# One load stream instead of two, query and key columns of group A sliced, and half of one modulation row after the routing

## The chip, the core and the metric

The kernel runs on one core of a Trainium2 chip. Its time is device microseconds of that core, the median of the runs shown. TensorE does the matmuls, VectorE (DVE), ScalarE (ACT) and GpSimd (POOL) the elementwise work, and SyncE (SP) issues the large loads.

## What is computed

A decoder layer on 256 tokens of 2048 features in float32: six modulation rows from c, a modulated RMSNorm, three groups of heads that share one input projection and one output projection, a second modulated norm, a mixture of 32 experts, a final norm.

```python
mod = (c_act @ ada_w[l] + ada_b[l])[:, None, :]
sh1, sc1, g1, sh2, sc2, g2 = jnp.split(mod, 6, axis=-1)
h = rmsnorm(x, norm1_g[l]) * (1.0 + sc1) + sh1
x = x + g1 * hybrid_mixer(h, w_in[l], ...)       # aq ak av | bq bk bv bz bb ba | cq ck cv, then @ w_out
h = rmsnorm(x, norm2_g[l]) * (1.0 + sc2) + sh2
x = x + g2 * hierarchical_moe(h, ...)            # group top-1, expert top-2 of 32
return rmsnorm(x, final_norm_g)
```

Group A is dilated attention (8 heads of 64), group B a gated delta rule (8 value heads of 128, with a causal convolution ahead of it), group C attention with sinks (8 heads, 2 key heads).

## The kernel before

All weights come in tiles of 128x2048 floats (1 MiB), each by one DMA that SP issues. A `Stream` (L114) holds a list of free slots in SBUF and a list of loads; a tile is loaded as soon as the program reaches a free slot, and tiles are used in the order of their loads. Each engine runs a fixed order, made at build time by a scheduler that takes instructions out of the program's order where it reckons that they are ready earlier; what stands earlier in the program goes first among ready ones.

Slices (L190 to L224, L298 to L388). The norm's two modulation rows sh1 and sc1 are made in six slices of 256 or 512 features (`ada_tile`, L298). A finished slice is turned into columns (`modulate`), x is normed and transposed into `hx` as a high and a low half (`input_rows`), and then the columns O_BQ to O_BZ of w_in are multiplied with this slice (`win_tile`, L357). Each weight tile is first split into halves: ACT casts it, DVE or POOL subtracts (`split`, L281). A product is three matmuls (`mm3`, L273). The first slice's result is copied to SBUF, those of the five later slices are added there by DVE (`evac`, L267). The 16 columns bb and ba are done with each slice as well (`gate_columns`), with the tokens stationary.

Pairs (L391 to L420). The other columns of w_in are done when all of `hx` is there: 256 columns in two tiles, with the sum kept in PSUM (`win_pair`). They are aq, ak, av, cq, ck, cv and bz; for av, bz and cv the tokens are stationary ("av", "tok"), for the others the weights ("chan").

Rows (L425 to L437). The other four modulation rows g1, sh2, sc2 and g2 need 16 tiles each (`row_tile`): eight matmul records per tile that share the array by column groups. `spread2` (L444) broadcasts a row over the partitions with two matmuls.

Two streams feed this: `st`, with three slots of its own plus one, carries slices, pairs and w_out, and after them the experts; `st2`, with the two slots of `side`, carries the rows (L453 to L482).

The middle (L936 to L953): the program has the delta rule (L676 to L884) first, then av, aq and ak with rows, attention A, the c columns with rows, attention C, the z columns with rows. Then x is loaded again, the delta rule's output is normed, gated and split (`delta_out`), and the output projection runs in two passes: tiles 0 and 3 of each column block (the attention groups) with the last rows, then tiles 1 and 2 (the delta rule's heads). The second pass also broadcasts g2 into `g2b` (L981 to L983), norms for the router and makes the logits.

Routing (L1031 to L1061) is a chain of small DVE operations, two matmuls for the slots' positions, and the gather of the first experts' tokens. The experts (L1239 on) then take 24 tiles a pair. From L943 on slots come free in steps: `side` and ring2's four give nine in all, ring3 gives three (after the output projection), the two tiles h2 (the routed rows before their split) two more.

Of the kernel before, what the change touches and what calls it, by code (L numbers as in the profile page):

```python
# [18 lines left out]
NB = 2  # L19
# [19 lines left out]

PAIRS = [c for a, e in ((O_AQ, O_BQ), (O_CQ, N_IN), (O_BZ, O_BB)) for c in range(a, e, 256)]  # L40

EARLY = ([("ada", s, k0, nk, q) for k0, nk in SLICES for s in range(2) for q in range(nk)]
         + [("b", k0, nk, c) for k0, nk in SLICES for c in range(O_BQ, O_BZ, 2048 // nk)]
         + [("pair", c, h) for c in PAIRS for h in range(2)]
# [4 lines left out]
def hybrid_moe(ctx: ExitStack, tc: tile.TileContext, x, c, norm1_g, norm2_g, early, ada_w, ada_b, w_bb,  # L49
# [129 lines left out]
    T.transpose(pt[:, 0:KT], csg, ident[0:KT, 0:KT])  # L179
    V.tensor_copy(csil[:, :, 3], pt[:, 0:KT])  # L180


# [21 lines left out]
    def win_items(j):  # L204
        k0, nk = SLICES[j]
        return [(early_load("b", k0, nk, c), lambda t, a=(k0, nk, c): win_tile(*a)(t)) for c in range(O_BQ, O_BZ, 2048 // nk)]

# [18 lines left out]
    for nk, r in ((4, 4), (2, 8)):  # L226
# [6 lines left out]
        for k0, n in SLICES:  # L233
            if n == nk:
# [21 lines left out]
    for tag, m0, n in CH:  # L256
        t = ep_tile(tag, n)
        for i in range(n):
            chan[m0 + i] = (t, i)
    av = ep.tile([P, NB, 512], F32, name="av", tag="av")  # L260
    tok = ep.tile([P, NB, 1024 + 16 + 128], F32, name="tok", tag="tok")
# [95 lines left out]
    def win_tile(k0, nk, c0):  # L357

        def chans(w, cc, m):

            h = hs[k0]
            p = bank("w")
            for u in range(2):
                for kt in range(nk):
                    mm3(p[:, 256 * u:256 * u + 256], [x[:, kt, cc + P * u:cc + P * (u + 1)] for x in w],
                        [x[:, kt] for x in h], kt == 0, kt == nk - 1)
            t, i = chan[m]
            evac(t[:, i:i + 2].rearrange("p m b t -> p (m b t)"), p, k0)

        def gate_columns():  # L370
            h = hs[k0]
            for b in range(NB):
                p = bank("w")
                for kt in range(nk):
                    mm3(p[:, 0:16], [x[:, kt, P * b:P * (b + 1)] for x in h], [x[:, k0 // P + kt] for x in wbb],
                        kt == 0, kt == nk - 1)
                evac(tok[:, b, K_BB:K_BB + 16], p[:, 0:16], k0)

        def f(t):
            t = t.rearrange("p (k n) -> p k n", k=nk)  # L380
            n = 1024 // nk
            for a in range(0, 2048 // nk, n):
                w = split(t[:, :, a:a + n], nk, 0)
                for z in range(0, n, 256):
                    chans(w, z, 8 + (c0 - O_BQ + a + z) // P)
            if c0 == O_BQ:
                gate_columns()
        return f  # L388
# [34 lines left out]
    rowp = {}  # L423

    def row_tile(i, kt):  # L425
        def f(t):
            if kt == 0:
                rowp[i] = bank("r", name="prow2")
            for g in range(4):
                mm(rowp[i][32 * g:32 * g + 32, :], csil[:, kt, 3 - i:35 - i], t[:, 512 * g:512 * (g + 1)],  # L430
                   start=(kt == 0), stop=(kt == 15))
            if kt == 15:
# [17 lines left out]

    rows_q = [(ada_rows(i, kt), row_tile(i, kt)) for i in range(4) for kt in range(KT)]

    st2 = Stream()  # L453

# [13 lines left out]
    rows_q = on(st2, rows_q)  # L468
    a_cols, c_cols, z_cols = ([x for c0 in range(a, e, 256) for x in on(st, win_pair(c0))]
                              for a, e in ((O_AQ, O_BQ), (O_CQ, N_IN), (O_BZ, O_BB)))  # L470
# [104 lines left out]
    st.retire(*spare)  # L575
    for s in side:
        st.retire(s, to=st2)
    st.grow((wk, "rx"))
# [13 lines left out]

    def swap_keys():
        kd = wk.tile([P, NB, P], F32, name="kswap")
# [67 lines left out]
    def attention(grp):  # L662
# [3 lines left out]
        for j in range(2):  # L666
            ms = (2 * j, 2 * j + 1)
            sd = [attn_scores(grp, m) for m in ms]
# [7 lines left out]
    def delta():  # L676
        def f4(t):
# [21 lines left out]

        conv(0)  # L700
        conv(1)

        bb = tok[:, :, K_BB:K_BB + 8]
        ba = tok[:, :, K_BB + 8:K_BB + 16]
# [77 lines left out]
        for b, hs, ts in units:  # L782
            p = bank("d")
            mm(p, identr, never[:, None, :].to_broadcast([P, 4, P]), start=True, stop=False)
            for i in range(4):
                h = hs.start + i
                mm(p[:, P * i:P * (i + 1)], gg[:, b, h:h + 1].to_broadcast([P, P]), tri, start=False, stop=True)
                S.activation(qk[:, b, h], p[:, P * i:P * (i + 1)], AF.Exp, bias=ngc[:, b, h:h + 1], scale=1.0)
        conv(2)
        conv(3)  # L790
        for b in range(NB):
            for q in range(2):
                tokens(vtok[:, b, 4 * q:4 * q + 4], cv[2 + q], b)
        R = [ep.tile([P, 8, P], F32, name="R", tag=f"bv{b}") for b in range(NB)]
        for b, hs, ts in units:
# [14 lines left out]
            V.tensor_tensor(Um[:, b, hs], ident[:, None, :].to_broadcast([P, 4, P]), Um[:, b, hs], op=ALU.subtract)  # L810
            transposed(Tm, Um, b, hs)
        for l in range(1, 7):

# [7 lines left out]
            for b, hs, _ in units:  # L821
# [18 lines left out]
            if l < 6:  # L840
                for b, hs, _ in units:
                    transposed(Um, Tm, b, hs)


# [357 lines left out]
    def squares(n):  # L1202
        for b in range(NB):
            if n == 3 and b:
                y = mp.tile([P, 1024], F32, name="sqv", tag="yal", bufs=1)[:, 0:512]
                V.scalar_tensor_tensor(y, x1[n][:, b], 0.0, x1[n][:, b], op0=ALU.add, op1=ALU.mult, accum_out=ss3[:, b, n:n + 1])
# [4 lines left out]
    def new_y(dt, s):  # L1211
        return tuple(mp.tile([P, 1024], dt, name=f"y{h}{s}", tag=f"y{h}{s}", bufs=1) for h in "ab")

# [23 lines left out]
    sl.gather_all()  # L1237
    behind = []
    for e in range(0, NE, 2):  # L1239
# [12 lines left out]
        if e == NE - 2:  # L1252
            hT.append(turned(1, hid[1]))
            break
        yh, yl = new_y(F32R, "h"), new_y(F32R, "l")
        for u in range(2):
# [16 lines left out]

    ys = new_y(F32, "h")
    for n in range(4):
# [13 lines left out]
    with tc.For_i(0, nov, 1):  # L1289
# [24 lines left out]
        sl.back(0)  # L1314
        ys = new_y(F32, "h")
        G.memset(ys[0][64:128], 0.0)
# [86 lines left out]
```

## Time and profile before

| | us |
|---|---|
| median of 3 runs | 1645.95 (1643.81 to 1646.33) |
| the profiled execution | 1645.27 |
| its span, first to last instruction | 1643.4 |
| TensorE busy | 1545.9 (94%) |
| VectorE, ScalarE, GpSimd busy | 672.1, 398.6, 182.8 |
| DMA | 573.76 MB, 349 GB/s over the span |

Times below are us from the start of the span. A busy TensorE is one with a matmul in flight; since matmuls overlap, the sum of single durations is more than the busy time. An idle time is put down to what ended it.

### The profile page before, as it was taken

What the parts mean: (1) busy time and instruction counts of PE and PEld (TensorE: products, weight loads), DVE (VectorE), ACT (ScalarE), POOL (GpSimd) and SP (SyncE); (2) the same over time, 40 slices, a digit from 0 to 9 for tenths busy, and PEclk for the clock granted to TensorE, in tenths of its full rate; (3) what the DMA queues carried; (4) which work ended last, traced back from release to release, by engine and by line L of the source; (5) the groups of instructions that cost most, each with busy time, mean ns of one, the idle gap of its engine ahead of it and who ended that gap; (6) DMA issues with size and microseconds to landing.
All of it is one profiled execution on the core that took longest, in us unless ns stands there. A gap on an engine that the chain in (4) does not pass through costs nothing. (4 is left out here: it accounts for less than half of the span.)

```text
span 1643.4 us, 23829 instructions
## 1 busy us (share of the span) xinstructions
PE 1545.9 (94%) x10064; PEld 945.0 (58%) x10064; DVE 672.1 (41%) x1138; ACT 398.6 (24%) x683; POOL 182.8 (11%) x104
## 2 busy tenths in 40 slices
PE   5899899999999999799999999999999999999895
PEld 3678767898877667544544545445445445445433
DVE  3534854334433544423432533344244234235324
ACT  3323563344345334210110110111011101101102
POOL 1111222352222432000000000000000000000000
PEclk8999999999999999799999999999999999999998
DMA  9986457634589894699999999999999999999995
GB/s 392 408 329 237 162 206 293 246 155 161 225 309 315 308 369 178 232 397 421 420 419 421 421 420 421 421 420 420 421 420 421 420 421 421 421 421 421 420 420 218
DMA packets 82437, 573.76 MB, mean 349 GB/s; under 512 B 9740, under 2 KB 10100, under 8 KB 13336
## 3 DMA queue, kind: packets, MB, share of 16 engines
q1 hardware_dynamic: 82080, 572.02, 86.6%
q8 instruction: 81, 1.33, 0.3%
q10 hardware_dynamic: 248, 0.19, 0.0%
q14 instruction: 28, 0.23, 0.0%
HBM read 570.07 MB, written 2.10 MB: 348 GB/s over the span
## 5 line engine op out<-in xcount | busy, mean ns | idle before, releaser
L65 PE MATMUL u<-ring,xg 128*64 128x512 f32 x2048 | 485.9, 604 | 7.8 <-DMA ring<-in_expert_gu_dram 7.8
L65 PEld LDWEIGHTS u<-ring,xg 128*64 128x64 f32 x2048 | 134.3, 137 | 236.1 <-issue 190.5
L65 PE MATMUL d<-ring,hidT 128*64 128x256 f32 x2048 | 238.1, 382 | 10.5 <-DMA ring<-in_expert_dn_dram 8.9
L65 PE MATMUL w<-hx,stg 128*128 128x256 f32 x1392 | 197.1, 293 | 9.8 <-ACT stg L289 3.1
L65 PEld LDWEIGHTS w<-hx,stg 128*128 128x128 f32 x1392 | 176.6, 194 | 41.8 <-issue 24.3
L65 PEld LDWEIGHTS d<-ring,hidT 128*64 128x64 f32 x2048 | 144.0, 137 | 90.9 <-issue 10.3
L290 POOL TENSOR_TENSOR stg<-ring,stg 128x1024 fp32r<-128x1024 f32 x53 | 128.3, 2421 | 410.5 <-ACT stg L289 367.3
L289 ACT CAST stg<-ring 128x1024 fp32r<-128x1024 f32 x116 | 121.2, 1047 | 187.7 <-PE w L65 152.4
L1190 DVE TENSOR_TENSOR xt<-xt,s 128x512 f32<-128x512 f32 x120 | 82.6, 688 | 165.2 <-PE s L65 164.4
L290 DVE TENSOR_TENSOR stg<-ring,stg 128x1024 fp32r<-128x1024 f32 x63 | 82.2, 1306 | 104.5 <-ACT stg L289 103.7
L1174 DVE SCALAR_TENSOR_TENSOR z<-d,gs,g2b 64x512 f32<-64x512 f32 x120 | 90.0, 750 | 76.1 <-PE d L65 74.2
L65 PE MATMUL prow<-ring,csil 128*32 128x512 f32 (+1 forms) x896 | 113.3, 566 | 0.3 <-DVE csil L180 0.3
L1272 POOL TENSOR_TENSOR xf<-xt,fgb 128x1024 f32<-128x1024 f32 x1 | 2.4, 2377 | 954.9 <-SPq L1289 954.9
L1107 DVE TENSOR_TENSOR xg<-g,sh2c 128x512 f32<-128x512 f32 x64 | 43.6, 691 | 136.8 <-PE u L65 75.7
L65 PEld LDWEIGHTS w<-stg,hx 128*128 128x128 f32 x672 | 83.6, 189 | 22.3 <-issue 18.0
L65 PE MATMUL w<-stg,hx 128*128 128x256 f32 (+1 forms) x672 | 96.1, 288 | 0.0
L1146 ACT ACTIVATE hid<-u 64x512 f32<-64x512 f32 x32 | 18.9, 590 | 286.7 <-PE u L65 276.5
L65 PEld LDWEIGHTS s<-yah,wt 128*128 128x128 f32 x120 | 22.6, 188 | 97.6 <-issue 58.8
L1177 ACT CAST yah<-z 64x512 fp32r<-64x512 f32 x60 | 37.0, 617 | 166.8 <-DVE z L1174 166.8
L1147 DVE TENSOR_TENSOR hid<-hid,u 64x512 f32<-64x512 f32 x32 | 22.1, 690 | 134.0 <-ACT hid L1146 133.8
L65 PE MATMUL g<-oh,h2hi 128*128 128x256 f32 x256 | 70.2, 307 | 5.5 <-DVE xg L1107 4.8
L1121 ACT CAST wt<-t 128x512 fp32r<-128x512 f32 x16 | 9.4, 587 | 233.7 <-PE s L65 222.6
(387 smaller groups left out, 1704.6 us busy)
## 6 DMA issues: line engine op xcount, KB each, us to landing
ring<-in_expert_gu_dram SPq DMA_DIRECT2D x256, 1024.0 KB, 19.8
ring<-in_expert_dn_dram SPq DMA_DIRECT2D x128, 1024.0 KB, 19.8
ring<-in_early_dram SPq DMA_DIRECT2D x90, 1024.0 KB, 8.2
ring<-in_ada_w_dram SPq DMA_DIRECT2D x64, 1024.0 KB, 5.7
xt<-in_x_dram SPq DMA_DIRECT2D x8, 512.0 KB, 6.3
out_dram<-xt SPq DMA_DIRECT2D x8, 256.0 KB, 4.4
fgb<-in_final_norm_g_dram SPq DMA_DIRECT2D x1, 1024.0 KB, 19.8
rw<-in_router_w_dram SPq DMA_DIRECT2D x1, 320.0 KB, 5.2
```

The lines of the kernel that those rows point to most:

```text
L65: return T.matmul(o, lhsT, rhs, start=start, stop=stop, skip_group_check=True)
L289: S.copy(hi, src)
L290: (G if nsplit[0] % GS[part] == GS[part] - 1 else V).tensor_tensor(lo, src, hi, op=ALU.subtract)
L1107: V.tensor_tensor(self.xg[:, 2 * q:2 * q + 2, 0:w], p[:, 0:2 * w].rearrange("p (k s) -> p k s", k=2), sh2c.rearrange("p n k -> p (n k)")[: ...
L1121: S.copy(self.wt.rearrange("p h b t -> p (h b t)"), p)
L1146: S.activation(hid[64:128], p[0:64], AF.Silu)
L1147: V.tensor_tensor(hid[0:64], hid[64:128], p[64:128], op=ALU.mult)
L1174: V.scalar_tensor_tensor(o.rearrange("p (n j) -> p n j", n=m), pd[q, 0:256 * m].rearrange("p (n j) -> p n j", n=m), gs[q, h, u:u + 1], g2h ...
L1177: S.copy(ys[h][q, c], o)
L1190: V.tensor_tensor(x1[n][:, b], x1[n][:, b], p, op=ALU.add)
L1272: G.tensor_tensor(xf, x1[0], fgb[:, None, 0:512].to_broadcast([P, NB, 512]), op=ALU.mult)
```

## The change

- `PAIRS`, `SLICED`, `CH`, `KINDS`: aq and ak (1024 columns, 8 tiles) are done in the slices with the b columns; the pairs are av, the c columns and z. cv is done with the weights stationary like cq and ck, and transposed to tokens in `swap_keys`.
- `gate_columns`: the 16 weight columns are stationary and 256 tokens move; the result `bbT` is transposed once, in the delta rule.
- One stream `st` keeps the slots of both: six from the last slices on. Column tiles, row tiles and the pieces of both attentions are merged into one list `fill` of 82 entries, and the delta rule takes an even share of it at each of its 24 `tick()` calls, the last of which stands at the end of its sixth level, ahead of its last part.
- Of the fourth row (g2) 8 of its 16 tiles are done as before; the other 8 stand in the load order behind w_out and ahead of the experts, and are multiplied after the routing's code, into a new PSUM bank, with a copy `csil2` of their stationary columns. The broadcast of g2 moves into the first expert's loop (`behind`).
- The two y tiles become 128x2x1024 tiles of a pool of their own, whose SBUF serves as two more slots once, before their first use.

```diff
-PAIRS = [c for a, e in ((O_AQ, O_BQ), (O_CQ, N_IN), (O_BZ, O_BB)) for c in range(a, e, 256)]
+PAIRS = [c for a, e in ((O_AV, O_BQ), (O_CQ, N_IN), (O_BZ, O_BB)) for c in range(a, e, 256)]
+SLICED = [(O_BQ, O_BZ), (O_AQ, O_AV)]
...
-          ("bv0", 16, 4), ("bv1", 20, 4), ("cq0", 24, 2), ("cq1", 26, 2), ("ck", 28, 1)]
+          ("bv0", 16, 4), ("bv1", 20, 4), ("cq0", 24, 2), ("cq1", 26, 2), ("ck", 28, 1), ("cv", 29, 1)]
...
-    KINDS = [(O_AQ, O_AV, "chan", 0), (O_AV, O_BQ, "av", 0), (O_BQ, O_BZ, "chan", 8), (O_BZ, O_BB, "tok", K_BZ),
-             (O_CQ, O_CV, "chan", 24), (O_CV, N_IN, "tok", K_CV)]
+    KINDS = [(O_AV, O_BQ, "av", 0), (O_BZ, O_BB, "tok", K_BZ), (O_CQ, N_IN, "chan", 24)]
...
         def gate_columns():
             h = hs[k0]
-            for b in range(NB):
-                p = bank("w")
-                for kt in range(nk):
-                    mm3(p[:, 0:16], [x[:, kt, P * b:P * (b + 1)] for x in h], [x[:, k0 // P + kt] for x in wbb],
-                        kt == 0, kt == nk - 1)
-                evac(tok[:, b, K_BB:K_BB + 16], p[:, 0:16], k0)
+            p = bank("w")
+            for kt in range(nk):
+                mm3(p[0:16, 0:256], [x[:, k0 // P + kt] for x in wbb], [x[:, kt] for x in h], kt == 0, kt == nk - 1)
+            evac(bbT, p[0:16, 0:256], k0)
...
-    rows_q = [(ada_rows(i, kt), row_tile(i, kt)) for i in range(4) for kt in range(KT)]
-    st2 = Stream()
+    rows_q = [(ada_rows(i, kt), row_tile(i, kt)) for i in range(4) for kt in range(KT) if i < 3 or kt < 8]
...
-    for s, load, _ in a_cols + c_cols + z_cols + on(st, w_items) + rows_q:
-        s.add(load)
+    fill = merge(a_cols + merge(c_cols, [0] * 8) + merge(z_cols, [1] * 8), rows_q[0:48])
+    for x in fill:
+        if isinstance(x, tuple):
+            st.add(x[1])
+    for n in range(4):
+        for _, load, _ in on(st, w_items[2 * n:2 * n + 2]) + rows_q[48 + 2 * n:50 + 2 * n]:
+            st.add(load)
+    for load, _ in w_items[8:]:
+        st.add(load)
+    for kt in range(8, KT):
+        st.add(ada_rows(3, kt))
...
-    ob_f4 = delta()
-    use(merge(a_cols, rows_q[0:24]))
-    attention(0)
-    use(merge(c_cols, rows_q[24:36]))
-    attention(1)
-    use(merge(z_cols, rows_q[36:56]))
+    parts = [attention(grp) for grp in range(2)]
+    ticks, taken = 24, [0, 0]
+    def tick():
+        taken[0] += 1
+        while taken[1] < len(fill) * taken[0] // ticks:
+            x = fill[taken[1]]
+            taken[1] += 1
+            if isinstance(x, tuple):
+                use([x])
+            else:
+                next(parts[x])
+    ob_f4 = delta(tick)
...
         wout_part(n, (0, 3), g1hl, ...)
-        use(rows_q[56 + 2 * n:56 + 2 * n + 2])
-    st.grow(*side)
+        use(rows_q[48 + 2 * n:48 + 2 * n + 2])
...
         wout_part(n, (1, 2), g1hl, ep.tile([P, 512], F32, name="g1s", tag="ak0"))
-        pg = bank("w")
-        spread2(pg, g1hl, 3, n)
-        S.copy(g2b[:, ns], pg)
...
+    yp = ctx.enter_context(tc.tile_pool(name="yp", bufs=1, side="right", reuse_waits="tile"))
+    for t in ("yh", "yl"):
+        st.grow((yp, t))
+        st.retire((yp, t))
...
     st.grow(*((cst, f"h2{b}") for b in range(NB)))
+    p = bank("s", 1)
+    for kt in range(8):
+        t = st.get()
+        for g in range(4):
+            mm(p[32 * g:32 * g + 32, :], csil2[:, kt, 0:32], t[:, 512 * g:512 * (g + 1)], start=(kt == 0), stop=(kt == 7))
+        st.done()
+    g2r = mp.tile([P, 512], F32, name="g2r", tag="hid", bufs=1)
+    V.tensor_tensor(g2r, mrow, p, op=ALU.add)
+    g2hl = halves(*(mp.tile([P, 512], F32R, name="g2hl", tag="z") for _ in range(2)), g2r)
+    def spread_g2(n):
+        p = bank("s", 1)
+        spread2(p, g2hl, 3, n)
+        S.copy(g2b[:, 512 * n:512 * (n + 1)], p)
...
-    behind = []
+    behind = [lambda n=n: spread_g2(n) for n in range(4)]
```

## Rows read from the trace of the kernel before

**Rows 1.** Busy time by stage: stretch, length, TensorE, weight loads, DVE, ACT, POOL; clock; DMA.
```profile
40.00:100.00 60.00, 54.95 (x418) 44.07 (x417) 28.20 (x55) 16.84 (x29) 7.13 (x3) 0.91 0.90 365
100.00:160.00 60.00, 59.42 (x525) 49.17 (x524) 26.32 (x42) 20.79 (x27) 9.74 (x5) 1.00 0.81 310
160.00:240.00 80.00, 72.00 (x519) 56.63 (x510) 59.44 (x101) 44.46 (x65) 21.29 (x11) 0.96 0.50 173
240.00:443.00 203.00, 203.00 (x1651) 170.41 (x1649) 76.93 (x143) 82.81 (x158) 69.09 (x41) 1.00 0.56 210
443.00:535.00 92.00, 92.00 (x707) 69.53 (x706) 33.31 (x62) 45.47 (x103) 24.35 (x11) 1.00 0.88 316
535.00:600.00 65.00, 64.45 (x324) 39.90 (x323) 31.60 (x33) 22.54 (x27) 23.86 (x10) 1.00 0.85 318
600.00:661.00 61.00, 61.00 (x291) 46.34 (x291) 25.56 (x36) 26.05 (x38) 19.01 (x8) 1.00 0.60 235
661.00:720.00 59.00, 48.79 (x236) 27.00 (x234) 21.63 (x65) 12.58 (x21) 0.24 (x1) 0.86 0.76 294
720.00:1600.00 880.00, 844.41 (x5071) 412.73 (x5070) 336.45 (x530) 101.82 (x166) 0.00 (x0) 0.99 1.01 420
```

**Rows 2.** Waits of TensorE from 40 to 240 us: total, times, longest.
```profile
PE w L65 <- ACT stg L289: 3.1, 2, 2.7
...
```

**Rows 3.** Waits of TensorE from 240 to 661 us.
```profile
PE d L907 <- DVE ob L903: 0.5, 1, 0.5
```

**Rows 4.** Expert loads that SP issues: start, time to the last one's end, count.
```profile
647.45 38.22 SPq L191 DMA_DIRECT2D ring<-in_expert_gu_dram  x8
687.06 0.33 SPq L191 DMA_DIRECT2D ring<-in_expert_dn_dram  x1
```

**Rows 5.** TensorE in order of time, 448 to 454 us: start, length, count.
```profile
448.36 1.64 PE L65 MATMUL w<-hx,stg 128*128 128x256 f32 x12
449.83 2.79 PE L65 MATMUL w<-stg,hx 128*128 128x128 f32 x24
452.55 1.07 PE L65 MATMUL prow<-ring,csil 128*32 128x512 f32 x8
453.55 0.65 PE L65 MATMUL a<-ck,ident 128*64 128x256 f32 x4
```

**Rows 6.** TensorE in order of time, a row's broadcast at 648 us.
```profile
648.37 0.72 PE L65 MATMUL w<-g1hl,identr 32*128 32x512 f32 x2
649.02 0.50 PE L65 MATMUL w<-stg,bq 128*128 128x512 f32 x1
```

**Rows 7.** TensorE in order of time, gate columns and what follows, twice.
```profile
61.96 1.40 PE L65 MATMUL w<-wbb,hx 128*128 128x16 f32 x12
...
63.29 1.06 PE L65 MATMUL prow<-ring,csil 128*32 128x512 f32 x8
...
83.22 2.56 PE L65 MATMUL w<-wbb,hx 128*128 128x16 f32 x12
```

**Rows 8.** TensorE in order of time, routing gap: positions, then the gather's first matmul.
```profile
675.06 1.06 PE L65 MATMUL t<-Ae,before 128*128 128x32 f32 x4 [6.55 <-DVE Ae L1049]
...
677.33 0.58 PE L65 MATMUL g<-oh,h2hi 128*128 128x256 f32 x1 [0.78 <-DVE oh L1093]
```

**Rows 9.** Groups of DVE instructions, 40 to 240 us: the add of a slice's result.
```profile
L271 DVE TENSOR_TENSOR bv<-bv,w 128x512 f32<-128x512 f32 x20 | 13.6, 686 | 28.2 <-PE w L65 28.2
```

**Rows 10.** In order of time: the delta rule's last part and its output.
```profile
396.46 1.15 PE L65 MATMUL d<-Um,t 128*64 128x64 f32 x16
...
444.00 0.67 DVE L880 TENSOR_TENSOR ob<-ob,d 128x512 f32<-128x512 f32 x1
...
536.58 6.73 DVE L903 TENSOR_TENSOR ob<-ob,tok 128x1024 f32<-128x1024 f32 x2
...
551.37 0.68 DVE L910 TENSOR_TENSOR bv<-d,bv 128x512 fp32r<-128x512 f32 x1
```

**Rows 11.** Busy time of 660 to 680 us, columns as in rows 1.
```profile
660.00:680.00 20.00, 9.79 (x48) 8.14 (x47) 14.52 (x45) 8.43 (x15) 0.24 (x1) 0.65 0.67 262
```

More of the change, by code (lines that the diff above doesn't have):

```diff
@@ L38 @@
 SLICES = [(0, 2), (256, 2), (512, 4), (1024, 4), (1536, 2), (1792, 2)]
-PAIRS = [c for a, e in ((O_AQ, O_BQ), (O_CQ, N_IN), (O_BZ, O_BB)) for c in range(a, e, 256)]
+PAIRS = [c for a, e in ((O_AV, O_BQ), (O_CQ, N_IN), (O_BZ, O_BB)) for c in range(a, e, 256)]
+SLICED = [(O_BQ, O_BZ), (O_AQ, O_AV)]
 EARLY = ([("ada", s, k0, nk, q) for k0, nk in SLICES for s in range(2) for q in range(nk)]
-         + [("b", k0, nk, c) for k0, nk in SLICES for c in range(O_BQ, O_BZ, 2048 // nk)]
+         + [("b", k0, nk, c) for k0, nk in SLICES for a, e in SLICED for c in range(a, e, 2048 // nk)]
          + [("pair", c, h) for c in PAIRS for h in range(2)]
@@ L180, in hybrid_moe @@
     V.tensor_copy(csil[:, :, 3], pt[:, 0:KT])
+    csil2 = cst.tile([P, 8, 36], F32, name="csil2")
+    V.tensor_copy(csil2, csil[:, 8:16])
     def early_load(*key):
@@ L205, in win_items @@
         k0, nk = SLICES[j]
-        return [(early_load("b", k0, nk, c), lambda t, a=(k0, nk, c): win_tile(*a)(t)) for c in range(O_BQ, O_BZ, 2048 // nk)]
+        return [(early_load("b", k0, nk, c), lambda t, a=(k0, nk, c): win_tile(*a)(t)) for s, e in SLICED for c in range(s, e, 2048 // nk)]
     def on(s, items):
@@ L259, in hybrid_moe @@
             chan[m0 + i] = (t, i)
+    bbT = ep.tile([P, 256], F32, name="bbT")[0:16]
     av = ep.tile([P, NB, 512], F32, name="av", tag="av")
@@ L425, in row_tile, with on_pe @@
     def row_tile(i, kt):
-        def f(t):
+        def on_pe(t):
             if kt == 0:
@@ L430, in f @@
                 mm(rowp[i][32 * g:32 * g + 32, :], csil[:, kt, 3 - i:35 - i], t[:, 512 * g:512 * (g + 1)],
-                   start=(kt == 0), stop=(kt == 15))
-            if kt == 15:
+                   start=(kt == 0), stop=(kt == (7 if i == 3 else 15)))
+        def f(t):
+            on_pe(t)
+            if kt == (7 if i == 3 else 15):
                 V.tensor_tensor(mrow, mrow, rowp.pop(i), op=ALU.add)
@@ L466, in use @@
                 tc.keep_in_program_order(nc.sync.dma_start(*small_loads.popleft()))
-    rows_q = on(st2, rows_q)
+    rows_q = on(st, rows_q)
     a_cols, c_cols, z_cols = ([x for c0 in range(a, e, 256) for x in on(st, win_pair(c0))]
-                              for a, e in ((O_AQ, O_BQ), (O_CQ, N_IN), (O_BZ, O_BB)))
+                              for a, e in ((O_AV, O_BQ), (O_CQ, N_IN), (O_BZ, O_BB)))
     w_items = [(early_load("out", n, q), None) for qs in ((0, 3), (1, 2)) for n in range(4) for q in qs]
-    for s, load, _ in a_cols + c_cols + z_cols + on(st, w_items) + rows_q:
-        s.add(load)
+    fill = merge(a_cols + merge(c_cols, [0] * 8) + merge(z_cols, [1] * 8), rows_q[0:48])
[9 more added lines that the diff above has]
+        st.add(ada_rows(3, kt))
     for e in range(0, NE, 2):
@@ L575, in hybrid_moe @@
     st.retire(*spare)
-    for s in side:
-        st.retire(s, to=st2)
     st.grow((wk, "rx"))
@@ L593, in swap_keys @@
     def swap_keys():
+        p = bank("a")
+        for b in range(NB):
+            T.transpose(p[:, P * b:P * (b + 1)], head(29)[:, b], ident)
+        S.copy(tok[:, :, K_CV:K_CV + 128], p[:, 0:256].rearrange("p (b n) -> p b n", b=NB))
         kd = wk.tile([P, NB, P], F32, name="kswap")
@@ L667, in attention @@
             ms = (2 * j, 2 * j + 1)
-            sd = [attn_scores(grp, m) for m in ms]
+            sd = []
+            for m in ms:
+                sd.append(attn_scores(grp, m))
+                yield
             pair = (ep_tile(f"cq{j}", 2, F32R), clo[:, 2 * j:2 * j + 2]) if grp else \
@@ L673, in attention, with delta @@
                 attn_values(grp, m, *sd[i])
-    def delta():
+                yield
+    def delta(tick):
         def f4(t):
@@ L700, in delta @@
         conv(0)
+        tick()
         conv(1)
+        tick()
+        pt = bank("d")
+        for b in range(NB):
+            T.transpose(pt[:, 16 * b:16 * (b + 1)], bbT[:, P * b:P * (b + 1)], ident[0:16, 0:16])
+        V.tensor_copy(tok[:, :, K_BB:K_BB + 16], pt[:, 0:32].rearrange("p (b n) -> p b n", b=NB))
         bb = tok[:, :, K_BB:K_BB + 8]
@@ L788, in delta @@
                 S.activation(qk[:, b, h], p[:, P * i:P * (i + 1)], AF.Exp, bias=ngc[:, b, h:h + 1], scale=1.0)
+            tick()
         conv(2)
+        tick()
         conv(3)
+        tick()
         for b in range(NB):
@@ L811, in delta @@
             transposed(Tm, Um, b, hs)
+            tick()
         for l in range(1, 7):
@@ L828, in delta @@
                 S.copy(ys[-1], p[:, 0:256])
+            tick()
             for (b, hs, _), y in zip(units, ys):
@@ L842, in delta @@
                     transposed(Um, Tm, b, hs)
+            tick()
         ktok = ep.tile([P, 4, P], F32, name="ktok", tag="bv0")
@@ L935, in hybrid_moe @@
     later(rbias[:, 8:40], row_bcast(router_expert_b, 32))
-    ob_f4 = delta()
-    use(merge(a_cols, rows_q[0:24]))
-    attention(0)
-    use(merge(c_cols, rows_q[24:36]))
-    attention(1)
-    use(merge(z_cols, rows_q[36:56]))
+    parts = [attention(grp) for grp in range(2)]
[10 more added lines that the diff above has]
+    ob_f4 = delta(tick)
+    assert taken == [ticks, len(fill)]
     x1 = x_tiles()
@@ L1204, in squares @@
             if n == 3 and b:
-                y = mp.tile([P, 1024], F32, name="sqv", tag="yal", bufs=1)[:, 0:512]
+                y = new_y(F32, "yl")[0][:, 0:512]
                 V.scalar_tensor_tensor(y, x1[n][:, b], 0.0, x1[n][:, b], op0=ALU.add, op1=ALU.mult, accum_out=ss3[:, b, n:n + 1])
@@ L1211, in new_y @@
     def new_y(dt, s):
-        return tuple(mp.tile([P, 1024], dt, name=f"y{h}{s}", tag=f"y{h}{s}", bufs=1) for h in "ab")
+        t = yp.tile([P, 2, 1024], dt, name=s, tag=s)
+        return t[:, 0], t[:, 1]
     ovn, ovs, ove = small("ovn", [P, NE]), small("ovs", [P, NE]), small("ove", [P, NE])
@@ L1254, in hybrid_moe @@
             break
-        yh, yl = new_y(F32R, "h"), new_y(F32R, "l")
+        yh, yl = new_y(F32R, "yh"), new_y(F32R, "yl")
         for u in range(2):
@@ L1272, in scaled @@
         G.tensor_tensor(xf, x1[0], fgb[:, None, 0:512].to_broadcast([P, NB, 512]), op=ALU.mult)
-    ys = new_y(F32, "h")
+    ys = new_y(F32, "yh")
     for n in range(4):
@@ L1314, in hybrid_moe @@
         sl.back(0)
-        ys = new_y(F32, "h")
+        ys = new_y(F32, "yh")
         G.memset(ys[0][64:128], 0.0)
```

2 lines of the change are left out of this document (1 added, 1 removed).

## The prediction

> **What bounds the kernel now.** I read the span by stages first: what TensorE and the DMA engines do in each stretch [rows 1]. The reader is to see two kernels in one. From 720 to 1600 us the DMA engines move 420 GB/s at full share: a 1 MiB tile of 1.0486 MB takes 2.497 us there, and nothing that the engines do shortens it. From 240 to 661 us it is the reverse: TensorE has 420.45 busy us of 421 at the full granted clock (1.00) while the DMA runs at 210 to 318 GB/s. The waits of TensorE say the same: in 240 to 661 us the one listed wait is 0.5 us [rows 3]. Before that, from 40 to 240 us, TensorE idles 60 - 54.95 + 60 - 59.42 + 80 - 72.00 = 13.6 us, and a granted clock of 0.91 and 0.96 costs some 60 x 0.09 + 80 x 0.04 = 8.6 us more [rows 1]; the longest listed one is 3.1 us on the split [rows 2]. So the end of the kernel is the moment from which the DMA engines are never idle again, plus the tiles then left at 2.497 us, plus a tail that the change leaves alone. That moment comes after the front, and the front is as long as TensorE's work.
>
> A matmul's busy time overlaps its neighbour's, so I price TensorE work from start to start in a full stretch: 12 matmuls of 256 columns from 448.36 to 449.83 (0.1225 each), 24 of 128 columns from 449.83 to 452.55 (0.113 each), one row tile (8 records) from 452.55 to 453.55, 1.00 us [rows 5].
>
> [...]
>
> **The change part by part: TensorE's work in the front.**
> Rows: 8 of the 64 row tiles leave the front for the routing gap: -8 x 1.00 = -8.0 us [rows 5].
> g2's broadcast: four pairs of 512-column matmuls leave the output projection's second pass; a pair takes 648.37 to 649.02, 0.65 us [rows 6]: -2.6 us. They return inside the first expert, where the experts' stream sets the pace.
> cv: before, 16 k-tiles x 3 x 2 token blocks = 96 matmuls of 128 columns at 0.113 = 10.8 us; after, 48 of 256 columns at 0.1225 = 5.9. Two added transposes, and two for the gate columns, at about 0.113 each, take back 0.5: net -4.4 us [rows 5].
> Gate columns: 96 matmuls with 16 moving columns, 12 of them from 61.96 to 63.29, 0.111 each [rows 7], 10.7 us; after, 48 with 256 moving columns and 16 weights. That form is not in the trace; its nearest rows are 0.111 (narrow) and 0.1225 (wide), 5.3 to 5.9 us. I take the wide one, as the moving side is the same: -4.8 us.
> Sum: 8.0 + 2.6 + 4.4 + 4.8 = 19.8 us less TensorE work.
>
> aq and ak move from pairs to slices: 8 tiles of 48 matmuls each, 48 x 0.1225 = 5.9 us a tile, 47 us from behind the delta rule's start to ahead of it. The work is the same, but each of the five later slices must add into SBUF: 20 more DVE adds of 128x512 at 686 ns [rows 9], 13.7 us on a DVE that is busy 59.44 of 80 us at the end of that stage [rows 1]. What they buy is cover: TensorE gets half as much projection work again for each modulated slice, exactly where it lost 22 us. Bounds: none of it (DVE becomes the wait) to some 12 us, half; in the stretch to 100 us the DMA already runs at 365 GB/s, so not all can go. I take 5 us gained.
>
> One stream in place of two, pieces by ticks: after 24 steps of the delta rule all column tiles, 48 row tiles and both attentions must have been issued in program order. Today the delta rule stands ahead of them and they only fill its stalls. Per TensorE nothing changes while anything is ready. Between the delta rule's start and the output projection there now lie 18 column tiles (106 us) and 48 rows (48 us) against 26 and 56, and the delta rule with attention, which today share the 295 us from 240 to 535 [rows 1]. Loads: 66 tiles x 2.497 = 165 us, well under that stage, so six slots in one order suffice unless a row blocks a column tile; SP's queue is in order, so such a tile would hold up all behind it. Exposed stalls: from none to some 15 us; TensorE has 0.5 us of them now. I take 4 us lost.
>
> So wout's end, 661 us in this profile, comes 19.8 + 5 - 4 = 20.8 us earlier.
>
> **What the DMA does with it.** Before, the nine slots fill with expert tiles during the second pass; after 661 us come three new slots, two that hold the routed rows, then one for each tile that TensorE eats. The queue issues 8 tiles from 647.45 to 685.67 and the next at 687.06 [rows 4]; 661 to 720 us has 294 GB/s of 420, a loss of 59 x (1 - 294/420) = 17.7 us [rows 1]. After, eight of the nine slots hold row tiles, so eight more tiles are still to come at that point, 8 x 2.497 = 20.0 us; but the two new slots in the y tiles and the eight slots that the rows give back keep the DMA busy through the gap. Without any idle time the loss of 17.7 us is paid back against 20.0: +2.3 us net. This is why moving rows out of TensorE's way does not bring all of its 8 us.
>
> The idle that may remain: rd's three and the y tiles' two loads last from 661 to about 661 + 2 + 5 x 2.5 = 675.5, the two of h2 to 680.5; the first row slot must be free by then. TensorE waits 6.55 us for the routing before 675.06 and starts gathering at 677.33 [rows 8], so the rows fit into it at 1.00 us. [...] Bounds 0 to 8 us, I take 1.5.
>
> [...]
>
> **Sum.** 1645.95 - 20.8 + 2.3 + 1.5 = 1628.95, so 1629.0 us. The profiled execution took 1645.27 us with a span of 1643.4; it stands 0.7 us under the median, which changes no term.
>
> **The rivals.**
> The delta rule loses its cover (slower). All ticks stand before its last part: from 396.46 to 444.00 its chain of four units runs, and its output needs 15 us more (gating from 536.58, where bz ends the wait today, to the last split at 552.05) [rows 10]. The only work left to hide that is the first pass of wout, 65 us today with its rows [rows 1]. For it: that work stands behind the chain in program order. Against it: TensorE is full today although its filler, too, stands behind. If half of those 62 us, less some 14 of the chain's own matmuls (an estimate from 120 of them at 0.113), stays bare, 24 us are lost: 1629.0 + 24 = 1653. It decides from 17 us on.
> TensorE is not the bound: the splits feed it at the pace of ACT and DVE, and fewer matmuls leave the front where it is. Nothing is gained but the later rows: 1645.95 + 3.8 = 1649.8. Against it: ACT 82.81 and DVE 76.93 busy us of 203 [rows 1].
> The front gains more: 12 us of the early loss, no new stall, no idle DMA: 1645.95 - 31.8 + 2.3 = 1616.5. For it: 22 us are there to be had.
> A row in the gap holds up the routing by 8 us: 1629 + 6.5 = 1635.5; inside the forecast's range.
>
> **How the numbers follow.** Forecast 0.70 (1618 to 1642), delta rule bare 0.13, TensorE not the bound 0.07, front gains more 0.10. From 1616 to 1645 us lies all of the forecast and most of the last case: 0.8. About 0.2%, 3.3 us, is what a measurement of this kernel can tell from no change. Faster takes the first and the last case, 0.80; the rival at 1649.8 lies on the edge and is shared: same 0.06, slower 0.14.
>
> **What would show it.** Right: the matmul count falls by some 100; TensorE stays full from about 200 us to the end of wout; that end lies near 640 us; the DMA is at full share from there on, without the dip at 680 us; the eight row tiles stand between the last logits and the gather. Wrong: waits of TensorE on the delta rule's tiles or on the ring; a DMA dip in the gap as deep as today's; an end of wout later than 650 us.

## The result and the profile after

The changed kernel takes 1633.2 us (median of 4 runs, 1629.66 to 1635.92), the kernel before beside it 1646.06 us; the ratio is 0.9925, 95% interval 0.9911 to 0.994. The forecast was 1629.0, range 1616 to 1645. The profiled execution of after has a span of 1631.7 us, 11.7 less than before. In what follows "before" and "after" stand for the two kernels, and e1 to e12 for the runs of the table below. One of e3's nine runs took 3542.87 us, for a reason that is not on record, and is left out of e3's ratio.

The stages of after, columns as in [rows 1], same stretches:

```profile
40.00:100.00 60.00, 58.59 (x469) 44.85 (x468) 29.84 (x58) 22.79 (x33) 9.56 (x4) 1.00 0.96 392
100.00:160.00 60.00, 60.00 (x514) 50.70 (x513) 26.52 (x38) 20.74 (x25) 11.91 (x5) 1.00 0.80 293
160.00:240.00 80.00, 75.39 (x600) 65.42 (x602) 55.36 (x93) 37.83 (x48) 17.18 (x7) 0.96 0.54 194
240.00:443.00 203.00, 201.00 (x1537) 155.19 (x1529) 81.02 (x171) 97.80 (x199) 66.05 (x37) 0.99 0.64 249
443.00:535.00 92.00, 89.79 (x654) 66.98 (x652) 35.44 (x55) 35.53 (x74) 28.29 (x17) 1.00 0.65 248
535.00:600.00 65.00, 61.08 (x262) 42.10 (x262) 34.44 (x46) 23.58 (x30) 21.05 (x10) 0.95 0.62 236
600.00:661.00 61.00, 58.48 (x300) 41.44 (x302) 32.92 (x67) 26.53 (x43) 13.49 (x7) 0.94 0.59 218
661.00:720.00 59.00, 56.78 (x328) 27.93 (x318) 17.67 (x41) 11.45 (x17) 0.00 (x0) 1.00 1.01 419
720.00:1600.00 880.00, 838.99 (x5055) 407.47 (x5052) 332.85 (x527) 97.98 (x161) 0.00 (x0) 1.00 1.01 420
```

Three things to see. The early stages hold more matmuls at a higher clock (469 in 40 to 100 us at 1.00, against 418 at 0.91). The dip of 661 to 720 us is gone: 419 GB/s against 294. And 240 to 600 us, where [rows 1] shows TensorE full, now has idle time and fewer matmuls. The matmul count falls from 10064 to 9972.

The loads that SP issues after the output projection, in order of time as in [rows 4]:

```profile
584.66 50.48 SPq L192 DMA_DIRECT2D ring<-in_ada_w_dram  x8
641.36 24.08 SPq L195 DMA_DIRECT2D ring<-in_expert_gu_dram  x16
670.46 27.44 SPq L195 DMA_DIRECT2D ring<-in_expert_dn_dram  x8
```

Eight row tiles take the slots that held experts before; then 16 expert tiles are issued within 24 us, where before 8 took 38.

TensorE in the routing's gap of after, as in [rows 8]:

```profile
653.75 8.99 PE L67 MATMUL s<-ring,csil 128*32 128x512 f32 x56
662.67 0.63 PE L67 MATMUL t<-Ae,before 128*128 128x32 f32 x4
```

Seven of the eight row tiles fill the wait of 6.55 us that [rows 8] shows, at 1.28 us each, and the positions come 1.4 us after their input (VectorE ends it at 661.05 + 0.22).

**A measure for what follows.** A busy TensorE says too little here, so I price its work: each matmul of the trace at the median start-to-start distance of its form, row tiles at 0.125 us a record (about half of it for records of 256 columns). A stretch less its priced work is lost time. Records can be missing: two kernels with the same work, before and e3, differ by 1.3 us (563.1 and 561.8). The choice of the medians matters more: one common price list for all kernels, or a list for each, moves the loss of 240 to 500 us by up to 4 us, so a smaller difference there is not read. The front's end is the start of the output projection's last matmul. Two profiles with the same order of instructions (e1_g1_early and e12_g1_early_shifted) differ by 2.4 us in it, so one profile is no more precise than that. It may be less so: the runs of before alone spread from 1639.1 to 1648.9 us. Medians from different sessions are not compared, the ratios to the kernel before are.

| kernel | lost in 40-240 us | 240-500 | 500-600 | front's end, us | tiles landed by 720 us | span, us | ratio (95%) |
|---|---|---|---|---|---|---|---|
| before | 36.1 | 14.0 | 4.9 | 660.3 | 184.8 | 1643.4 | 1 |
| after | 21.5 | 26.3 | 18.7 | 646.9 | 189.7 | 1631.7 | 0.9925 (0.9911-0.994) |
| e5_before_less_work | 34.1 | 19.8 | 4.6 | 651.6 | 189.5 | 1631.3 | 0.9938 (0.9919-0.9958) |
| e3_before_slices | 16.5 | 37.1 | 6.2 | 664.1 | 183.2 | 1647.4 | 1.0042 (1.0027-1.0057) |
| e10_no_slices | 30.8 | 17.1 | 16.2 | 649.4 | 188.5 | 1634.5 | 0.9953 (0.9935-0.9971) |
| e1_g1_early | 20.2 | 27.6 | 12.0 | 638.4 | 192.6 | 1625.2 | 0.9889 (0.9868-0.991) |
| e4_no_ticks | 21.4 | 30.0 | 7.1 | 642.2 | 191.4 | 1627.6 | 0.9881 (0.9861-0.9902) |
| e7_g1_early_no_ticks | 21.6 | 29.9 | 7.3 | 643.4 | 190.9 | 1629.2 | 0.9893 (0.9874-0.9913) |
| e2_rows_front | 20.3 | 25.3 | 24.4 | 665.3 | 184.1 | 1646.6 | 1.003 (1.0014-1.0046) |
| e6_rows_front_56_8 | 20.5 | 19.0 | 19.0 | 644.3 | 191.8 | 1628.6 | 0.9912 (0.9895-0.9929) |
| e11_rows_front_g1_early | 19.0 | 18.7 | 13.1 | 636.5 | 194.5 | 1621.0 | 0.9885 (0.9866-0.9903) |
| e8_gap_12_rows | 21.3 | 26.6 | 17.8 | 641.0 | 188.3 | 1623.7 | 0.9889 (0.9871-0.9907) |
| e9_gap_12_g1_early | 23.0 | 27.5 | 14.1 | 638.7 | 188.9 | 1623.0 | 0.9873 (0.9854-0.9893) |
| e12_g1_early_shifted | 22.5 | 28.0 | 12.2 | 640.8 | 191.8 | 1616.1 | 0.9831 (0.9811-0.9851) |

Span plus 2.495 us for each tile landed by 720 us is 2104 to 2107 us in eleven of these kernels (before 1643.4 + 461.1, after 1631.7 + 473.3). So what a front is worth can be read at 720 us, and nothing behind it differs. The other three, e8, e9 and e12, give 2093 to 2095; the last section is about them.

### The profile page after: what moved, and what is told of

It reads as the page before. It is cut to its first block, busy times and chain, and to the rows that moved or that the text cites. A ratio compares the mean times of both kernels' runs of the same rounds, so it can differ in the third digit from the quotient of the medians.

```text
span 1631.7 us, 23636 instructions
## 1 busy us (share of the span) xinstructions
PE 1538.1 (94%) x9972; PEld 926.7 (57%) x9972; DVE 675.9 (41%) x1160; ACT 399.4 (24%) x680; POOL 175.5 (11%) x101
## 5 line engine op out<-in xcount | busy, mean ns | idle before, releaser
L67 PE MATMUL w<-hx,stg 128*128 128x256 f32 x1440 | 190.3, 286 | 3.3 <-DVE bk L275 1.3
L294 POOL TENSOR_TENSOR stg<-ring,stg 128x1024 fp32r<-128x1024 f32 x50 | 120.6, 2412 | 371.5 <-ACT stg L293 329.0
L1236 ACT CAST yh<-z 64x512 fp32r<-64x512 f32 x120 | 74.0, 617 | 267.9 <-DVE z L1233 267.9
L67 PEld LDWEIGHTS s<-yh,wt 128*128 128x128 f32 x240 | 44.9, 187 | 94.7 <-issue 60.3
L67 PE MATMUL w<-stg,hx 128*128 128x256 f32 x576 | 86.4, 300 | 4.4 <-DVE aq L275 1.8
L67 PEld LDWEIGHTS w<-stg,hx 128*128 128x128 f32 x576 | 75.4, 198 | 17.0 <-issue 8.9
L1237 DVE TENSOR_TENSOR yl<-z,yh 64x512 fp32r<-64x512 f32 x120 | 82.2, 685 | 3.1
L67 PE MATMUL s<-yh,wt 128*128 128x256 f32 x240 | 75.1, 333 | 5.6 <-ACT yh L1236 5.6
## 6 DMA issues: line engine op xcount, KB each, us to landing
ring<-in_expert_gu_dram SPq DMA_DIRECT2D x256, 1024.0 KB, 19.8
ring<-in_expert_dn_dram SPq DMA_DIRECT2D x128, 1024.0 KB, 19.8
fgb<-in_final_norm_g_dram SPq DMA_DIRECT2D x1, 1024.0 KB, 19.8
```

The source lines that it names most:

```text
L67: return T.matmul(o, lhsT, rhs, start=start, stop=stop, skip_group_check=True)
L294: (G if nsplit[0] % GS[part] == GS[part] - 1 else V).tensor_tensor(lo, src, hi, op=ALU.subtract)
L1236: S.copy(ys[h][q, c], o)
L1237: V.tensor_tensor(yl[h][q, c], o, ys[h][q, c], op=ALU.subtract)
```

## The experiments

**Less work alone, on the kernel before.** cv as a channel column, and the gate columns turned:

```diff
-                    mm3(p[:, 0:16], [x[:, kt, P * b:P * (b + 1)] for x in h], [x[:, k0 // P + kt] for x in wbb],
-                        kt == 0, kt == nk - 1)
+                mm3(p[0:16, 0:256], [x[:, k0 // P + kt] for x in wbb], [x[:, kt] for x in h], kt == 0, kt == nk - 1)
...
-             (O_CQ, O_CV, "chan", 24), (O_CV, N_IN, "tok", K_CV)]
+             (O_CQ, N_IN, "chan", 24)]
```

> The kernel before, with two parts of the change alone: the gate columns with 256 moving columns in place of two times 128, and cv as a channel column that is transposed later. By the prediction they take 4.8 + 4.4 = 9.2 us of TensorE work out of the front and change nothing else. Theory (TensorE's work is the bound of the front): 9 us faster than before, 1637 (1635 to 1640). Rival (the splits or the loads feed the front, so that fewer matmuls leave it where it is): 1645 to 1647 as before.

1633.54 us beside 1643.32 for before, 0.9938; the front ends 8.7 us earlier for 9.2 forecast. In the kernel before, the front's end follows TensorE's work, and the kernel's end follows the front's. The rival in which splits or loads feed the front has fallen. By the table the work itself shrinks by some 12 us, and 3.5 us of that come back as lost time, most of it in 240 to 500 us (19.8 against 14.0).

**Slices alone on the kernel before, and everything but the slices.**

```diff
-         + [("b", k0, nk, c) for k0, nk in SLICES for c in range(O_BQ, O_BZ, 2048 // nk)]
+         + [("b", k0, nk, c) for k0, nk in SLICES for a, e in SLICED for c in range(a, e, 2048 // nk)]
```

e3 adds this to the kernel before, with the kinds and pairs that go with it; e10 takes it out of the changed kernel.

> The kernel before, with one part of the change alone: aq and ak as slices beside b's in place of pairs. Theory (TensorE's early idle time is filled: the forecast took 5 us, the changed kernel's trace shows 13 us less loss in 40 to 200 us and some 6 us more in 200 to 320, where the delta rule's convolutions now wait for a later end of the slices): 5 to 8 us faster than before, ratio 0.995 to 0.997, about 1638 to 1641 beside 1646. Rival 1 (the added sums on VectorE and the later start of the delta rule give all of it back): within 2 us of before. Rival 2 (all 13 us stay): ratio 0.992.

> The changed kernel with aq and ak as pairs again, at the head of the pieces that the delta rule's steps take; nothing else undone. Theory (the slices only move TensorE's idle time: with each matmul priced at its start-to-start distance, the changed kernel loses 14.6 us less than before in 40 to 240 us and 12.3 us more in 240 to 500, and on the kernel before the slices alone cost 4 to 7 us): the loss in 40 to 240 us is back at 34 to 36 us, that of 240 to 500 falls to 14 to 18, and the kernel is 0 to 5 us faster than the changed one, 1628 to 1634. Rival (in one stream the slices pay, since the pieces left to the 24 steps load in time): slower than the changed kernel, 1638 to 1645.

e3: 1652.5 us, slower than before, 1.0042, which neither its theory nor a rival had. The early loss falls by 19.6 us and that of 240 to 500 us rises by 23.1. Two of its stages, columns as in [rows 1]:

```profile
240.00:300.00 60.00, 58.68 (x381) 44.81 (x381) 32.38 (x60) 36.88 (x65) 17.25 (x9) 0.91 0.63 235
300.00:360.00 60.00, 60.00 (x430) 42.53 (x429) 30.81 (x78) 23.44 (x49) 15.03 (x9) 1.00 0.69 251
```

and the same stretch of before:

```profile
300.00:360.00 60.00, 60.00 (x516) 52.98 (x515) 17.32 (x30) 22.13 (x44) 27.98 (x18) 1.00 0.55 207
```

A clock as low as before has early (0.91 in 40 to 100) stands at 240 to 300 here. Behind it TensorE is busy for 60.00 of 60 us in both kernels, with 430 matmuls in one and 516 in the other; priced, 51.6 and 59.5 us of work. e10 takes 1635.96 us, 0.9953, in neither the theory's range nor the rival's. The losses move the way that its theory had (30.8 early in place of 34 to 36, 17.1 later), but the front ends 2.5 us later, not earlier (about the precision of one profile). So the slices move idle time from the early stage behind the delta rule's start. What they bring on balance is small: a loss of 0.4% on the kernel before, a gain of about 0.3% in the change (0.9953 against 0.9925), at the edge of what these runs can tell, as the two intervals overlap a little.

**The bare stretch behind the delta rule.** In after, from 515 to 550 us, the waits of TensorE:

```profile
PE w L67 <- DVE t L445: 1.9, 1, 1.9
PE d L67 <- DVE t L901: 1.6, 2, 0.8
PE w L67 <- ACT g1s L960: 0.7, 1, 0.7
PE d L67 <- DVE t L895: 0.6, 1, 0.6
```

and ScalarE in order of time:

```profile
534.63 0.62 ACT L444 CAST t<-mrow 128x512 fp32r<-128x512 f32 x1 [12.69 <-DVE so L930]
...
538.62 0.58 ACT L960 COPY g1s<-w 128x512 f32<-128x512 f32 x1 [1.29 <-PE w L67]
```

The first output tile of the pass has its sums in two of the three banks "w" by 518 us and waits there for g1's broadcast. The tile `mrow` that holds g1's row was last written by the add at 502.87 us (for another row; g1's own add was at 315.8), but its first half is cast at 534.63, because it takes the scratch tiles behind the delta rule's output. Until then no second output tile starts (TensorE's next matmul on a split tile stands at 539.25), and the splits and the loads stop with it: ScalarE casts no tile of the ring between 518.20 and 546.30 us, and SP issues no load between 531.56 and 551.07.

```diff
     assert taken == [ticks, len(fill)]
+    g1hl = halves(*(tmp.tile([P, 2, 256], F32, name="ct", tag="ct", bufs=2).rearrange("p u s -> p (u s)").bitcast(F32R)
+                    for _ in range(2)), mrow)
...
     delta_out(*ob_f4)
-    g1hl = halves(scratch(dt=F32R), scratch(dt=F32R), mrow)
```

> The changed kernel, with g1's two halves made right behind the delta rule's last step and ahead of its output, in two tiles of their own; nothing else differs. Theory (TensorE's front sets the end, and what the forecast missed is the stretch of 520 to 548 us, where the first pass of the output projection could not cover the delta rule's last part because g1's row stood behind the delta rule's output): the first pass runs inside that stretch, TensorE is busy over 18 of 20 us in 520 to 540 (15.04 now), the end of the second pass moves up by 6 to 10 us and with it the end: 1623 to 1627 us. Rival (that stretch is slack, since something else, the loads at 75 GB/s in 540 to 560 us or the delta rule's own chain, ends last anyway): within 3 us of the changed kernel's 1633.2, 1630 to 1636.

1627.04 us, 0.9889 against 0.9925. The cast stands at 502.53 us, no wait of TensorE is left in 515 to 550, and 500 to 600 us reads:

```profile
500.00:600.00 100.00, 97.09 (x478) 68.72 (x478) 59.62 (x74) 36.99 (x50) 38.01 (x18) 1.00 0.67 261
```

against this in after:

```profile
500.00:600.00 100.00, 93.87 (x455) 65.36 (x448) 53.75 (x66) 33.76 (x45) 33.99 (x17) 0.97 0.64 244
```

**No ticks**, and both edits together:

```diff
-    ob_f4 = delta(tick)
-    assert taken == [ticks, len(fill)]
+    ob_f4 = delta(lambda: None)
+    for _ in range(ticks):
+        tick()
```

> The changed kernel, with the whole delta rule ahead of the column tiles, rows and attention pieces in program order, as in the kernel before; one stream, same pieces, same order among them. Theory (TensorE is full whenever work is ready, so the mixing in 24 steps buys nothing there, but it delays the delta rule's last part to 500 to 540 us, where little is left to cover it): the delta rule ends 60 us or more earlier, the bare stretch is gone, the loss from 500 to 600 us falls from 24 to under 14 us, and the end comes 4 to 10 us earlier: 1623 to 1629 us. Rival 1 (the mixing is what lets one stream of six slots work; without it column tiles stand behind rows or attention in the queue): slower than 1640 us with TensorE waiting for ring tiles. Rival 2 (neither matters): 1630 to 1636.

> The changed kernel with both edits of e1_g1_early and e4_no_ticks. Theory (both cure the same thing, the delta rule's last part with too little beside it): about as fast as the better one alone, 1623 to 1627 us, ratio to before 0.987 to 0.989. Rival (two separate losses, 6 us and 7 us, that add): 1620 us, ratio 0.984 to 0.985.

e4: 1625.07 us, 0.9881. The delta rule's last sum stands at 496.47 us in place of 535.26 (444.00 in [rows 10]) and the loss of 500 to 600 us falls from 18.7 to 7.1. One stream of six slots does not need the mixing: from 515 to 600 us no wait of TensorE on the ring is listed. The loss in 240 to 500 us stays (30.0), so the ticks are not its cause. e7: 1628.99 us, 0.9893, no better than either: both edits cure the same stretch, as expected.

**Rows back in the front.** The rows in the routing's gap go, and all 64 stand in the front. In e2 four stand behind each part of the first pass:

```diff
-    rows_q = [(ada_rows(i, kt), row_tile(i, kt)) for i in range(4) for kt in range(KT) if i < 3 or kt < 8]
+    rows_q = [(ada_rows(i, kt), row_tile(i, kt)) for i in range(4) for kt in range(KT)]
...
-        use(rows_q[48 + 2 * n:48 + 2 * n + 2])
+        use(rows_q[48 + 4 * n:48 + 4 * n + 4])
```

In e6 56 stand among the delta rule's steps and two behind each part, beside e2:

```diff
-    fill = merge(a_cols + merge(c_cols, [0] * 8) + merge(z_cols, [1] * 8), rows_q[0:48])
+    fill = merge(a_cols + merge(c_cols, [0] * 8) + merge(z_cols, [1] * 8), rows_q[0:56])
...
-        use(rows_q[48 + 4 * n:48 + 4 * n + 4])
+        use(rows_q[56 + 2 * n:56 + 2 * n + 2])
```

e11 is e6 with the edit of e1.

> The changed kernel, with the eight row tiles of the routing's gap put back into the front (all 64 there, four behind each of the four parts of the first pass); g2's broadcast stays in the first expert. Theory (the prediction's accounting): the front is 8.0 us longer, and the 3.8 us that eight later tiles cost the DMA come back: 4.2 us slower than the changed kernel, 1637 (1634 to 1641). Rival 1 (the front's length does not set the end): 3.8 us faster, 1629. Rival 2 (the rows cost nothing in the front because they fill stalls that are bare now): within 2 us of 1633, and TensorE's idle time in 520 to 600 us shrinks by what they take.

> All 64 row tiles in the front as in e2_rows_front, but 56 of them among the pieces of the delta rule's steps and two behind each of the four parts of the first pass, as in the kernel before; g2's broadcast in the first expert. Theory (the prediction's accounting holds: 8.0 us of TensorE in the front against 3.8 us of the DMA; e2_rows_front lost more because four rows stand ahead of the next output tile in the one queue of loads): 4 us slower than the changed kernel, 1637 (1634 to 1641), and ACT has no waits of 8 to 10 us on output tiles in 545 to 600 us. Rival (eight rows in the front cost some 15 us wherever they stand there): 1645 to 1650.

> e6_rows_front_56_8 with g1's halves made early, as in e1_g1_early. Theory (rows among the steps of the delta rule run in TensorE's idle time there, so all 64 in the front cost nothing, and the bare stretch of 520 to 540 us is a separate loss): 6 to 8 us faster than e6_rows_front_56_8, 1623 to 1626, the front's end near 637 us. Rival (with more rows in place the bare stretch is not what ends the front): 1629 to 1632.

e2: 1648.68 us, slower than the kernel before; no theory had that. ScalarE in e2:

```profile
558.67 1.99 ACT L293 CAST stg<-ring 128x1024 fp32r<-128x1024 f32 x2 [8.10 <-DMA ring<-in_early_dram]
...
579.84 1.99 ACT L293 CAST stg<-ring 128x1024 fp32r<-128x1024 f32 x2 [10.13 <-DMA ring<-in_early_dram]
```

Four rows stand between each pair of output tiles and the next in the one queue of loads, so the next lands late and the split, then TensorE, wait for it (TensorE 8.7 us in three waits on ScalarE's casts, from 520 to 680 us). e6, with the rows elsewhere, has none of these: 1630.86 us, 0.9912. That is not 4 us slower than the change, as the accounting had it, but as fast or a little faster (0.9925 for the change). In 240 to 500 us e6 does 241.0 us of priced work where after does 233.7, in the same time: the eight rows ride in TensorE's idle time there, though it reads as busy for 258 of 260 us in after. e6 has the dip at the gap again, 18.2 us of the DMA's time, and eight fewer tiles to come. e11: 1624.37 us, 0.9885: g1 early brings 0.27% here and 0.36% in e1, so the two effects are separate as far as these runs can tell, and all rows in the front with g1 early is as fast as e1.

**Twelve rows in the gap**, one behind each part of the first pass (e8), and the same with the edit of e1 (e9):

```diff
-    csil2 = cst.tile([P, 8, 36], F32, name="csil2")
+    csil2 = cst.tile([P, 12, 36], F32, name="csil2")
...
-    for kt in range(8):
+    for kt in range(12):
```

> The changed kernel with twelve row tiles in the routing's gap in place of eight, one behind each of the four parts of the first pass in place of two. Theory (the end is the moment from which the DMA is full plus 2.497 us for each tile still to come; with eight rows there is no dip left to pay for more): the front is 4 to 5 us shorter, four tiles more come behind it, 10.0 us, so 5 to 6 us slower than the changed kernel, 1638 to 1640. Rival 1 (the front's length alone counts): 1628 to 1630. Rival 2 (the front's last part waits for loads and not for TensorE, so that a row out of it saves more than 1.0 us, up to the 2.5 us of its load): as the changed kernel, within 2 us of 1633.

> e8_gap_12_rows with g1's halves made early, as in e1_g1_early. In e8_gap_12_rows the front (last matmul of the output projection) ended at 641.0 us and 188.3 tiles had landed by 720 us, 1.4 fewer than in the changed kernel, as the theory of the DMA has it; but its stream of experts ran at 425.9 GB/s where every other kernel's ran at 420, and that gave back some 11 us. Theory (the front ends 6 to 8 us earlier again, near 634 us, since the bare stretch of 520 to 540 us is the same; 191 tiles by 720 us). With the rate at 420, which would make the 426 a matter of that load of the program: 1627 to 1631 us, no better than e1_g1_early. Rival (the rate belongs to the order of tiles and slots that twelve rows make): 425 to 426 GB/s again and 1617 to 1621 us.

e8: 1627.18 us, 0.9889, where the theory had 1638 to 1640. Its front and its tiles follow the theory (5.9 us earlier, 1.4 tiles fewer at 720 us). The rate behind them does not, columns as in [rows 1]:

```profile
800.00:1500.00 700.00, 672.56 (x4073) 329.49 (x4068) 268.02 (x413) 80.35 (x132) 0.00 (x0) 1.00 1.01 426
```

e9: 1624.71 us, 0.9873, and 426 GB/s again. Its front ends at 638.7 us with 188.9 tiles landed, where the theory had 634 and 191, and the time is above the 1617 to 1621 us that the rival gave for this rate; why g1 early moves the front by only 2.3 us here (about the precision of one profile) is open. The rate belongs to the program, not to one load of it.

**The shift alone**, on e1_g1_early:

```diff
-    csil2 = cst.tile([P, 8, 36], F32, name="csil2")
+    csil2 = cst.tile([P, 12, 36], F32, name="csil2")[:, 0:8]
```

> e1_g1_early with one tile ahead of the ring made 576 bytes longer in every partition, as long as it is in the two kernels with twelve rows; nothing reads or writes the added part, and the order of instructions is the same on every engine. Two runs moved 425.9 GB/s where all others moved 419 to 420.5: e8_gap_12_rows and e9_gap_12_g1_early. They differ from the rest in their rows and in the addresses of the ring's slots in SBUF, which lie 576 bytes higher (nine of the fourteen then at a multiple of 512, and none before). Theory (the addresses do it): 425 to 426 GB/s from 800 to 1500 us and some 11 us less than e1_g1_early, 1615 to 1619 us, ratio to before 0.982 to 0.984. Rival (the order of rows and experts in the stream does it): 420 GB/s and 1625 to 1629 us, ratio 0.989.

1617.86 us, 0.9831, the fastest kernel here. Its row:

```profile
800.00:1500.00 700.00, 677.98 (x4115) 333.04 (x4114) 270.86 (x417) 80.99 (x133) 0.00 (x0) 1.00 1.01 426
```

and that of e1_g1_early:

```profile
800.00:1500.00 700.00, 669.99 (x4060) 327.53 (x4056) 267.38 (x412) 80.39 (x132) 0.00 (x0) 1.00 1.01 420
```

The 576 bytes do it, and with them the addresses; the order of rows and experts does not.

## Why the prediction was right, and where not

The sign, the rule for the end and the time (4.2 us over the forecast) hold. That the time came out so near is in part luck: two of its terms were far off, with opposite signs. The early gain was 10 us larger than taken, the new stalls 22 us larger, and the front ended 13.4 us earlier in place of 20.8. Of the signs that the prediction named for being wrong, one showed: waits of TensorE on the delta rule's tiles (those on `t` L901 and L895 above). Of those for being right, one failed: TensorE was not full to the end of wout.

- **The end is the moment from which the DMA is full, plus 2.497 us a tile.** Right: the sum of span and tiles under the table, 2104 to 2107 us in eleven kernels.
- **Less TensorE work, -19.8 us.** Priced by the trace the front's work falls from 563.1 to 538.4, 24.7 us. Other choices of the medians give 20 to 29 us, so the forecast's 19.8 is not refuted. The experiment on the gate columns and cv (e5) bears out its part of the sum: the front ends 8.7 us earlier for 9.2. The unseen form costs what the wide bound said: five of its matmuls from 211.08 to 211.68 us, 0.12 each.
- **Early idle time filled, +5 us.** Mis-sized: 14.6 us less is lost in 40 to 240 us, above the bound of 12. The early slices were not as load-bound as the 365 GB/s of [rows 1] made me think: the stretch runs at 392.
- **New stalls, -4 us.** This is the step that failed. 12.3 us more are lost in 240 to 500 us and 13.8 in 500 to 600, 26 in all, above the bound of 15. The working said that "nothing changes while anything is ready", and took TensorE for full from [rows 1] and [rows 3]. A busy TensorE there only means that a matmul was in flight. In 300 to 360 us e3 has 60.00 busy us with 86 fewer matmuls than before. The runs show where the lost time comes from: with aq and ak as pairs again (e10) the loss of 240 to 500 us is 17.1 in place of 26.3, so much of that part goes with the slices (in e3 they alone add 23.1), and with g1 early (e1) that of 500 to 600 is 12.0 in place of 18.7. Which wait makes the first part is not shown.
- **Busy time, and the rival that TensorE is not the bound.** From before to after, TensorE's busy time in 240 to 443 us goes from 203.00 to 201.00 while that of the weight loads goes from 170.41 to 155.19. Weight loads go with the priced work only in part: in 240 to 500 us e6 has 7.3 us more of it than after, but weight loads of 197.35 us against 198.90. For the kernel before, e5 refutes the rival (the front ends 8.7 us earlier); in the changed kernel e6 shows that more TensorE work between 240 and 500 us need not move the front's end (644.3 us against 646.9 in after).
- **The output projection's end.** 13.4 us earlier in place of 20.8, at 646.9 and not near 640, though before the 650 us that the prediction named as a sign of being wrong.
- **The DMA, +2.3 and +1.5.** Right. From the front's end to 720 us the DMA loses 18.7 us before and 1.1 after, against eight more tiles, 20.0: +2.4. The 1.5 us taken for the remaining idle time, with bounds of 0 to 8, were the author's estimate, which no run shows; what after shows in its place is the 1.1 us.
- **Eight rows out of the front, -8.0 us.** By e6 they cost nothing there, since they fill stalls. With the DMA's terms the move of the rows to the gap is worth nothing that these runs can tell (0.9912 against 0.9925). The shorter work of the gate columns and cv alone gives 0.9938 (e5), which these runs can't tell from the whole change's 0.9925. What the other parts add is not separated part by part, as they act on the same stalls.
- **The rival of the delta rule without cover.** It came true in part: 6 to 7 us of it (e1, e4), not 24. It did so by one late cast that held the banks, which the rival had not named, more than by a lack of work.
- **The rows in the gap.** The clock is 0.84 in 640 to 661 us and 1.00 behind it. In 660 to 680 us TensorE of after is busy for 20.00 of 20 us at 1.00, where [rows 11] has 9.79 at 0.65. At 1.28 us each the eight rows take some 10 us, against 8 at the 1.00 us each of the sum. They hold the routing up by 1.4 us; the 8 us of the rival were the author's estimate.

## What to carry to other kernels

Price TensorE's work from start to start, stretch by stretch, before calling it full: a stretch that reads busy for 60 of 60 us held an eighth less work than another (51.6 us in e3 against 59.5 in before, 300 to 360 us). When work moves ahead of a chain, ask what then covers the chain's last part, and look for the small late instruction (here one cast of a row) that holds the banks of the work meant to cover it. In one queue of loads the order of the tiles counts: the same 64 rows in the front gave 1.003 with four between the pairs of output tiles (e2) and 0.9912 with two (e6).

## What was not expected of the hardware

Moving eleven of the fourteen slots that the experts use up by 576 bytes in every partition (with whatever else stands behind the lengthened tile) raised the rate of the experts' stream from 420 to 426 GB/s. The time went from 0.9889 to 0.9831 of the kernel before, 9 us; at an equal front it would be some 11 us, by the sums of span and tiles under the table. In the traces an 8 KB packet takes 313 ns at the median from 800 to 1500 us in e1_g1_early and 309 in e12_g1_early_shifted. Nine slots then start at a multiple of 512 bytes, none before. Such a multiple alone does not explain it: five of the fourteen slots stay off one, and yet 95% of all packets are within 312 ns. Which address decides is open; no run here has another shift.
